# Two of the five column operands of a seven-product feed-forward stage, taken from turned blocks instead of being turned

## The chip, the cores and the metric

The kernel runs on one core of a Trainium2 chip. The metric is the device time of one execution in microseconds (us), the median of several runs. Engines are named as in the profile: PE (matrix products and transposes), DVE (elementwise, two inputs), ACT (elementwise, one input), POOL, and SP, which issues most transfers.

## What is computed

The reference is one layer of a streaming encoder on 1024 tokens of width 1024: a mixer (gated delta rule and a short convolution), then a feed-forward block, then a last norm. The change lies in the feed-forward block:

```
h = rms_norm(x, norm2_w) * (1.0 + scale2) + shift2
x = x + gate2 * ((silu(h @ w_gate) * (h @ w_up)) @ w_down)
```

All values are float32. A product is made of three passes in a 32-bit format that PE takes at one column per step ("fp32r"): each operand is split into a high part (rounded to fp32r) and a low part (the rest), and high by high, high by low and low by high are summed.

## The kernel before

**The stage.** `h @ w_gate` and `h @ w_up` are computed in 11 pairs `p`, each of 256 columns of the two weights. Within a pair the 2 by 2 block product (two halves of the 1024 inputs, two halves of the tokens) is done with seven products instead of eight, in the manner of Strassen and Winograd. The weights give A11, A12, A22 and the sums S1 to S4. The normed tokens, turned so that the inputs lie on partitions, give B11, B21, B22 and T1 to T4:

- T1 = B12 - B11, T2 = B22 - T1, T3 = B22 - B12, and T4 here is B21 - T2.
- The steps of a pair are in the table `STEPS` (line 44): X += A11 B11; Y += A12 B21; X += S2 T2; Z += S1 T1; X += S3 T3; Z += S4 B22; X += A22 T4.
- X, Y and Z are PSUM banks, one each for gate (`q` = 0) and up (`q` = 1). `run(p, s, q_)` (line 1798) issues step `s`: for each `q`, 4 blocks of 128 inputs times three passes, so 12 products of 128x512, or 24 for both `q`. Between the steps the banks are read out: `keep` copies a bank with ACT, `close` adds a bank to a kept copy on DVE, `silu` and `act` finish a block.

**How the B and T operands are made.** After the mixer, tokens lie on partitions in eight tiles `x2n[0..7]`, four for each half of the tokens. `norm_tile` norms a tile. `first_half` and `inner_half` (lines 1567, 1576) turn the first four tiles into B11 and B21: PE turns 128x128 blocks into a PSUM bank (four to a bank), ACT makes the high part, DVE the low part (`tr_split`, line 1543). `sums_x(i)` (line 1557) then makes, still on tokens, the sums of T1, T2, T3 and T4 of tile pair `i`, in place, with four DVE operations of 128x512. In the first pair, p = 0, `t_split(n, banks)` (line 1779) turns one of the operands T2, T1, T3, T4, B22 at a time: 16 transposes into four banks, then 4 ACT and 4 DVE operations. All eleven pairs use these operands.

**What sets the order.** From line 1492 on each engine takes its instructions in the order in which the code is written. Lines 2041 to 2085 are the first pair: PE's transposes stand between its steps, and the first pair's weight sums (`sum_n`), high parts (`cast`) and low parts (`low`; `mat` does both for both `q`) stand among them. High and low parts of weights lie in a ring of buffers (`slot`, line 1768). `W[1].load` (lines 2074, 2075) puts the second pair's weights on SP's queue, into space that the tiles `x2n` held.

Of the kernel before, what the change touches and what calls it, by code (L numbers as in the profile page):

```python
# [17 lines left out]
P = 128  # L18
HEAT = (4, 12, 20)
DMA_T = (1.8, 0.9)  # L20
D = 1024
KB = 8
NT = 8
HT = 512
# [22 lines left out]
A_IX = {n: i for i, n in enumerate(("A11", "A12", "S2", "S1", "S4", "S3", "A22"))}  # L47
# [4 lines left out]
def kernel(  # L52
# [25 lines left out]
    class Ordered:  # L78
# [18 lines left out]
    PE, DVE, ACT, POOL, SP = (Ordered(n, e) for n, e in (  # L97
        ("pe", nc.tensor), ("dve", nc.vector), ("act", nc.scalar), ("pool", nc.gpsimd), ("sp", nc.sync)))
# [7 lines left out]
    def nm(s):  # L106
        n_id[0] += 1
        return f"{s}_{n_id[0]}"
# [11 lines left out]
    class Banks:  # L120
# [68 lines left out]
    def dma(out, in_):  # L189
        SP.dma_start(out=out, in_=in_)  # L190
# [76 lines left out]
    for i, t in enumerate(x0):  # L267
        rs, sq, p0, p1 = norm_rs(t, sp, "n1")
# [274 lines left out]
    b2c = cst.tile([P, KB], F32, name="b2c", tag="b2c")  # L543
    db2 = cst.tile([P, 4], F32, name="db2", tag="db2")
# [921 lines left out]
    gp = x2p = b1p = None  # L1466
# [27 lines left out]
    allb = Banks([5, 6, 7, 3, 4, 0, 1, 2])  # L1494
# [4 lines left out]
    pe = seq  # L1499
# [4 lines left out]
    def bank_tile(b, name):  # L1504
        return psp.tile([P, HT], F32, name=nm(name), tag=f"b{b % 8}")
# [3 lines left out]
    x2n = list(x2)  # L1509
# [45 lines left out]
    tm = {}  # L1555

    def sums_x(i, which=(0, 1)):
        lo, hi = x2n[i], x2n[4 + i]
        if 0 in which:
            tm[i] = raw_t()  # L1560
            DVE.tensor_tensor(lo[:, 0:HT], hi[:, 0:HT], lo[:, 0:HT], ALU.subtract)
            DVE.tensor_tensor(tm[i], hi[:, HT:D], lo[:, 0:HT], ALU.subtract)
        if 1 in which:
            DVE.tensor_tensor(hi[:, 0:HT], hi[:, HT:D], hi[:, 0:HT], ALU.subtract)
            DVE.tensor_tensor(lo[:, HT:D], lo[:, HT:D], tm[i], ALU.subtract)

    def first_half(ks):
        for k in ks:
            H[k][0] = tr_split(lambda: h_slot(k, 0), [x2n[i][:, k * P:(k + 1) * P] for i in range(4)], allb.get("tr"), b2c[:, k:k + 1])

    HN = HT // 2
    tq = {n: hp_.tile([P, 2, 2, HN], F32R, name=n, tag=n) for n in ("q1", "q2", "q3")}

    fq = {}

    def inner_half(a):
# [5 lines left out]
        pa, pb = bank[4 + a], bank[6 + a]  # L1582
        if not fq:
# [68 lines left out]
    w_out_tile(5, 1)  # L1652
    keep_x2(5, (1,))
    inner_half(0)
    inner_half(1)
    early_load(0)
    early_load(1)
    sums_x(0)
# [24 lines left out]
    mp = m_ctx.__enter__()  # L1683
# [91 lines left out]
    B = {"B11": [H[k][0] for k in range(4)], "B21": [H[k][0] for k in range(4, 8)]}  # L1775
# [2 lines left out]

    def t_split(n, banks):
        for k in range(4):  # L1780
            def get():
# [5 lines left out]
            c0 = k * P + (HT if n in ("T4", "B22") else 0)  # L1787
            srcs = [tm[i][:, k * P:(k + 1) * P] if n == "T2" else
                    x2n[i + (4 if n in ("T3", "B22") else 0)][:, c0:c0 + P] for i in range(4)]
            col = {"T2": b2c, "B22": b2c, "T3": db2}.get(n)  # L1790
            off = 0 if n == "T3" else 4
            B[n][k] = tr_split(get, srcs, bank_tile(banks[k], "tr"), None if col is None else col[:, off + k:off + k + 1])
# [53 lines left out]
    def cc(p, n):  # L1846
        if p == 0 and n == "p1":
            c[p][n] = [cst.tile([P, HT], F32, name=nm("cc"), tag="ct"),
                       wst.tile([P, HT], F32, name=nm("cc"), tag="aacc", bufs=1)]
        else:  # L1850
# [190 lines left out]
    dma(x2_scr[7], x2[7])  # L2041
    run(0, 0)
    run(0, 1, (0,))
    W[0].sum_n("S1", (0,))
    W[0].sum_n("S2", (0,))
    keep(0, "p1", "X")
    W[0].cast("S2", 0)
    t_split("T2", (6, 7, 4, 5))
    W[0].low("S2", 0)
    run(0, 1, (1,))  # L2050
    W[0].sum_n("S1", (1,))
    W[0].sum_n("S2", (1,))
    W[0].cast("S2", 1)
    W[0].low("S2", 1)
    t_split("T1", (6, 7, 4, 5))
    close(0, "p1", "Y")
    silu(0, "p1")
    run(0, 2, (0,))
    act(0, "p1")
    dma(am_scr[0, A_IX["A11"]], c[0]["p1"][0])  # L2060
    t_split("T3", (6, 7, 4, 5))
    run(0, 2, (1,))
    W[0].mat("S1")
    t_split("T4", (6, 7, 2, 3))
    W[0].sum_n("S3")
    W[0].sum_n("S4")
    run(0, 3, (0,))
    W[0].mat("S3")
# [7 lines left out]
    keep(0, "u2", "X")  # L2076
    run(0, 3, (1,))
    run(0, 4)
    keep(0, "z5", "Z")
    W[0].mat("S4")  # L2080
    for s in (5, 6):
        if s == 5:
            W[0].mat("A22")
        run(0, s)
        block(0, s)
    for p in range(1, NP):
# [156 lines left out]
    for k, (n, i) in enumerate(slots):  # L2243
        ci, s = seq_d[n]
        ps = prod_d(ci, s, i)
# [80 lines left out]
```

## Time and profile before

| what | value |
|---|---|
| median of 3 runs | 1164.13 us (1163.93 to 1164.54) |
| the profiled execution | 1164.59 us |
| its span | 1162.5 us |
| PE busy in the span | 1152.4 us, 99% |
| DVE / ACT busy | 959.1 us (83%) / 563.1 us (48%) |
| the seven steps of the first pair | from 520.42 to 568.33 us in the span |

How to read it: the span runs from the first to the last instruction that the profile records; the execution's own time is 2.1 us longer. In a timeline, a row is a run of equal instructions: its start, the time from the first one's start to the last one's end, how many (x), and in square brackets the engine's idle time before it with what ended it. "acc" is a PSUM bank of X, Y or Z; "tr" a bank of transposes; "hl" a weight's high and low part; "S" and "R" weight sums and raw weights; "T" and "h" the split T and B operands ("h" also the split T1, which takes such a place); "cc" the kept copies; "raw" in the region of the change holds the T2 sums.

### The profile page before, as it was taken

How to read it: one execution, taken by the hardware profiler on the slowest of the kernel's cores; microseconds unless marked ns; L12 is line 12 of the kernel's file. 1: busy time of each engine (PE TensorE's matmuls, PEld its weight loads, DVE VectorE, ACT ScalarE, POOL GpSimd, SP SyncE). 2: the span in 40 equal slices, each digit the busy share in tenths (PEclk: the TensorE clock that was granted, in tenths of full speed). 3: DMA queues.
4: the chain of work that ended last, by engine and by line, in shares of the span. 5: the costliest groups of instructions: out<-in, count | busy, mean ns of one | idle time of the engine just before them, and what ended most of it. 6: DMA issues, size and time to landing. Idle time of an engine off the chain costs nothing.

```text
span 1162.5 us, 16907 instructions
## 1 busy us (share of the span) xinstructions
PE 1152.4 (99%) x5714; PEld 971.4 (84%) x5714; DVE 959.1 (83%) x1807; ACT 563.1 (48%) x1241; POOL 60.1 (5%) x100
## 2 busy tenths in 40 slices
PE   9999999999999999999999999999999999999997
PEld 7888888888888888888888888888888888888886
DVE  6899889899987898678787778777887797688676
ACT  6779633459634552325434433434434465443344
POOL 1110001002101010100000000000000000000002
PEclk9999999999999999999999999999999999999999
DMA  9823455534225455434264456445654599869403
GB/s 361 324 89 104 147 163 152 182 118 148 96 67 172 155 193 179 173 105 140 81 217 139 160 191 217 168 140 182 235 171 151 176 325 394 319 204 340 145 30 145
DMA packets 127542, 209.18 MB, mean 180 GB/s; under 512 B 20576, under 2 KB 45152, under 8 KB 127456
## 3 DMA queue, kind: packets, MB, share of 16 engines
q1 hardware_dynamic: 122080, 204.90, 51.4%
q10 hardware_dynamic: 5376, 3.21, 0.9%
q8 instruction: 45, 0.74, 0.3%
q14 instruction: 41, 0.34, 0.1%
HBM read 153.01 MB, written 55.05 MB: 179 GB/s over the span
## 4 chain that ended last, share of the span: by engine, by line
PE 93%; DVE 3%; ACT 2%; DMA 1%; issue 1%; SPq 0%; POOL 0%; ACTq 0%; DVEq 0%; POOLq 0%
PE acc L89 34%; PE acc L448 25%; PE dn L89 17%; PE o L448 4%; PE o L89 3%; PE A L448 1%; PE K L448 1%; DVE xo L90 1%; PE ab L448 1%; PE O L448 1%; PE kk L448 1%; DVE T L90 0%; PE qk L448 0%; DVE hl L90 0%; DMA raw<-in_w_ada_dram 0%
## 5 line engine op out<-in xcount | busy, mean ns | idle before, releaser
L448 PE MATMUL acc<-h,u 128*128 128x512 f32 x1200 | 298.6, 398 | 0.0
L448 PEld LDWEIGHTS acc<-h,u 128*128 128x128 f32 x1200 | 219.6, 188 | 42.2 <-issue 0.5
L89 PE MATMUL acc<-h,hl 128*128 128x512 f32 x576 | 135.3, 390 | 0.0
L89 PE MATMUL acc<-T,hl 128*128 128x512 f32 x552 | 131.3, 391 | 0.5 <-ACT cc L90 0.5
L89 PEld LDWEIGHTS acc<-h,hl 128*128 128x128 f32 x576 | 107.4, 188 | 21.8
L89 PEld LDWEIGHTS acc<-T,hl 128*128 128x128 f32 x552 | 102.3, 188 | 21.2 <-ACT cc L90 0.9
L89 PE MATMUL acc<-h,u 128*128 128x512 f32 (+1 forms) x480 | 91.8, 341 | 0.0
L90 DVE TENSOR_TENSOR xo<-xo,dn 128x512 f32<-128x512 f32 x84 | 57.1, 685 | 41.5 <-PE dn L89 34.2
L89 PE MATMUL dn<-h,h 128*128 128x512 f32 x396 | 90.7, 389 | 0.0
L89 PEld LDWEIGHTS acc<-h,u 128*128 128x128 f32 x480 | 78.3, 189 | 11.7
L89 PEld LDWEIGHTS dn<-h,h 128*128 128x128 f32 x396 | 74.4, 188 | 15.4
L448 ACT CAST u<-raw 128x512 fp32r<-128x512 f32 x66 | 40.6, 620 | 63.6 <-PE acc L448 62.3
L90 DVE TENSOR_TENSOR cc<-cc,acc 128x512 f32<-128x512 f32 x66 | 41.5, 647 | 32.1 <-PE acc L89 31.5
L448 DVE TENSOR_TENSOR u<-raw,u 128x512 fp32r<-128x512 f32 x82 | 56.1, 686 | 9.0 <-ACT u L448 8.8
L89 PE MATMUL acc<-T,u 128*128 128x512 f32 x240 | 56.0, 390 | 0.0
L90 ACT CAST hl<-S 128x512 fp32r<-128x512 f32 x44 | 25.3, 622 | 61.3 <-DVE S L90 61.3
L448 DVE SCALAR_TENSOR_TENSOR cv<-pr,cols_a,cv 128x512 f32<-128x512 f32 x72 | 53.4, 748 | 0.9 <-ACT cv L448 0.5
L90 ACT CAST h<-rw 128x512 fp32r<-128x512 f32 x57 | 32.7, 618 | 41.7 <-PE dn L89 34.6
L89 PEld LDWEIGHTS acc<-T,u 128*128 128x128 f32 x240 | 45.1, 188 | 9.3
L90 ACT ACTIVATE cc<-cc 128x512 f32<-128x512 f32 x33 | 20.9, 632 | 64.2 <-DVE cc L90 63.8
L90 ACT CAST u<-R 128x512 fp32r<-128x512 f32 (+1 forms) x60 | 34.1, 584 | 34.3 <-DVE R L90 34.2
L90 DVE TENSOR_TENSOR hl<-S,hl 128x512 fp32r<-128x512 f32 x44 | 28.5, 688 | 26.9 <-ACT hl L90 26.9
(370 smaller groups left out, 2137.8 us busy)
## 6 DMA issues: line engine op xcount, KB each, us to landing
raw<-in_w_in_dram SPq DMA_DIRECT2D x82, 256.0 KB, 3.2
am_scr<-cc SPq DMA_DIRECT2D x77, 256.0 KB, 4.5
raw<-in_w_ada_dram SPq DMA_DIRECT2D x56, 256.0 KB, 3.3
rw<-am_scr SPq DMA_DIRECT2D x55, 256.0 KB, 5.2
rw<-bm_scr SPq DMA_DIRECT2D x53, 256.0 KB, 5.3
bm_scr<-raw SPq DMA_DIRECT2D x51, 256.0 KB, 5.5
R<-in_w_gate_dram SPq DMA_DIRECT2D x22, 512.0 KB, 3.9
R<-in_w_up_dram SPq DMA_DIRECT2D x22, 512.0 KB, 5.3
```

Of the source, the lines that this page charges most:

```text
L89: return call(*a, **k)
L90: ins = call(*a, **k)
L448: ins = call(*a, **k)
```

## The change

T3 and T4 are no longer summed on tokens and turned. They are summed from operands that are turned anyway, since T3 = T2 - B11 and T4 = B21 - T2 hold for turned blocks as well.

- `keep_raw` (new, called in `first_half` and after `inner_half`): ACT copies the eight PSUM banks of the turned B11 and B21, without the shift, to SBUF: B11 by way of `kb` buffers (from which `sums_x` moves it on with another ACT copy), B21 into the right halves of `x2n[0..3]`.
- `sums_x`: two DVE operations of a tile pair instead of four, and that ACT copy.
- `t_split` only turns (T2, T1, B22); its ACT and DVE work is now in `t_turned`, which for T2 also copies the four turned banks to SBUF (into `tm`, the buffers of the T2 sums).
- `t_sums` makes T3 and T4 in SBUF (4 DVE operations each), `t_parts` splits them (4 ACT and 4 DVE operations each, as before, but out of SBUF).
- The first pair's weight sums S1, S2 and S4 are made for gate and up together ahead of the split parts, and the parts are made one `q` at a time with `part`.
- The copies of u2's start (`keep(0, "u2", "X")`) go to a buffer of their own and stand earlier; `act(0, "p1")`, and the store of its result, stand later, behind T4's parts.

```
     def sums_x(i):
         lo, hi = x2n[i], x2n[4 + i]
+        tm[i] = raw_t()
+        DVE.tensor_tensor(lo[:, 0:HT], hi[:, 0:HT], lo[:, 0:HT], ALU.subtract)
+        DVE.tensor_tensor(tm[i], hi[:, HT:D], lo[:, 0:HT], ALU.subtract)
+        ACT.copy(hi[:, 0:HT], b11[i])
+        kept[i] = hi[:, 0:HT]
-            DVE.tensor_tensor(hi[:, 0:HT], hi[:, HT:D], hi[:, 0:HT], ALU.subtract)
-            DVE.tensor_tensor(lo[:, HT:D], lo[:, HT:D], tm[i], ALU.subtract)
+    def keep_raw(ks, banks):
+        for k, ps in zip(ks, banks):
+            if k < 4:
+                b11.append(gp.tile([P, HT], F32, name=f"kb{k}", tag=f"Tt{k}", bufs=1))
+                ACT.copy(b11[k], ps)
+            else:
+                kept[k] = x2n[k - 4][:, HT:D]
+                ACT.copy(kept[k], ps)
...
+        if n == "T2":
+            for k in range(4):
+                ACT.copy(tm[k], t_ps[n, k][0])
+    def t_sums(n):
+        for k in range(4):
+            if n == "T3":
+                DVE.scalar_tensor_tensor(kept[k], tm[k], db2[:, k:k + 1], kept[k], ALU.add, ALU.subtract)
+            else:
+                DVE.tensor_tensor(tm[k], kept[4 + k], tm[k], ALU.subtract)
+    def t_parts(n):
+        for k in range(4):
+            t = B[n][k] = mp.tile([P, 2, HT], F32R, name=nm(n), tag=f"{n}_{k}", bufs=1)
+            split(kept[k] if n == "T3" else tm[k], t[:, 0], t[:, 1], DVE)
+    def part(n, q):
+        W[0].cast(n, q)
+        W[0].low(n, q)
```

The first pair's order is now the following (before: lines 2041 to 2085 above):

```
    run(0, 1, (0,))
    W[0].sum_n("S1")
    W[0].sum_n("S2")
    keep(0, "p1", "X")
    part("S2", 0)
    part("S2", 1)
    t_split("T2", (6, 7, 4, 5))
    t_turned("T2")
    part("S1", 0)
    run(0, 1, (1,))
    t_split("T1", (6, 7, 4, 5))
    part("S1", 1)
    t_turned("T1")
    close(0, "p1", "Y")
    run(0, 2)
    t_sums("T3")
    silu(0, "p1")
    keep(0, "u2", "X")
    W[0].sum_n("S3")
    part("S3", 0)
    t_parts("T3")
    run(0, 3, (0,))
    part("S3", 1)
    t_sums("T4")
    W[0].sum_n("S4")
    t_split("B22", (6, 7, 2, 3))
    part("S4", 0)
    t_turned("B22")
...
    W[1].load(0)
    W[1].load(1)
    run(0, 3, (1,))
    keep(0, "z5", "Z")
    run(0, 4)
    part("S4", 1)
    part("A22", 0)
    t_parts("T4")
    part("A22", 1)
    act(0, "p1")
    dma(am_scr[0, A_IX["A11"]], c[0]["p1"][0])
    for s in (5, 6):
        run(0, s)
        block(0, s)
```

What stands on the engines, at three places. **PE**, in the first pair behind the first four blocks of step 2 (X of gate += S2 T2). Before, 16 transposes follow (the first five are shown; `tr` is a PSUM bank, `x_4` to `x_6` and `h_1_982` are the second half's token tiles):

```order
L89 MATMUL acc_5446<-T_998_5501,hl_5494 128x512 x3
L89 MATMUL acc_5446<-T_1000_5509,hl_5494 128x512 x3
L89 MATMUL acc_5446<-T_1002_5517,hl_5494 128x512 x3
L89 MATMUL acc_5446<-T_1004_5525,hl_5494 128x512 x3
L89 MATMUL tr_5595<-ident,x_4_4587 128x128
L89 MATMUL tr_5595<-ident,x_5_4588 128x128
L89 MATMUL tr_5595<-ident,x_6_4589 128x128
L89 MATMUL tr_5595<-ident,h_1_982_5426 128x128
L89 MATMUL tr_5603<-ident,x_4_4587 128x128
```

And with the change:

```order
L89 MATMUL acc_5454<-T_1002_5530,hl_5504 128x512 x3
L89 MATMUL acc_5454<-T_1003_5533,hl_5504 128x512 x3
L89 MATMUL acc_5454<-T_1004_5536,hl_5504 128x512 x3
L89 MATMUL acc_5454<-T_1005_5539,hl_5504 128x512 x3
L89 MATMUL acc_5455<-T_1002_5530,hl_5507 128x512 x3
L89 MATMUL acc_5455<-T_1003_5533,hl_5507 128x512 x3
L89 MATMUL acc_5455<-T_1004_5536,hl_5507 128x512 x3
L89 MATMUL acc_5455<-T_1005_5539,hl_5507 128x512 x3
L89 MATMUL acc_5647<-h_1_1012_5584,hl_5546 128x512 x3
```

The up half of step 2 follows at once, and step 3 behind it; the same holds where T4 was turned. **DVE**, ahead of the two additions of `close(0, "z5", "X")`, which read the X banks that step 6 goes on to add to. Before:

```order
L90 SCALAR_TENSOR_TENSOR h_1_1043_5730<-tr_5725,b2c,h_1_1043_5730 128x512
L90 TENSOR_TENSOR hl_5785<-R_5441,hl_5785 128x512
L90 TENSOR_TENSOR hl_5788<-R_5442,hl_5788 128x512
L90 TENSOR_TENSOR hl_5791<-R_5441,hl_5791 128x512
L90 TENSOR_TENSOR hl_5794<-R_5442,hl_5794 128x512
L90 TENSOR_TENSOR cc_5782<-cc_5782,acc_5446 128x512
L90 TENSOR_TENSOR cc_5782<-cc_5782,acc_5447 128x512
```

And with the change:

```order
L90 TENSOR_TENSOR hl_5754<-R_5450,hl_5754 128x512
L90 TENSOR_TENSOR hl_5757<-R_5449,hl_5757 128x512
L90 TENSOR_TENSOR T_1039_5760<-raw_5246,T_1039_5760 128x512
L90 TENSOR_TENSOR T_1040_5763<-raw_5314,T_1040_5763 128x512
L90 TENSOR_TENSOR T_1041_5766<-raw_5395,T_1041_5766 128x512
L90 TENSOR_TENSOR T_1042_5769<-raw_5437,T_1042_5769 128x512
L90 TENSOR_TENSOR hl_5772<-R_5450,hl_5772 128x512
L90 TENSOR_TENSOR cc_5500<-cc_5501,cc_5500 128x512
L90 TENSOR_TENSOR cc_5727<-cc_5727,acc_5454 128x512
L90 TENSOR_TENSOR cc_5727<-cc_5727,acc_5455 128x512
```

T4's four low parts and `act(0, "p1")` (`cc_5500`) now stand ahead of the two additions. **ACT**, behind the turning of T2. Before, the next weight part follows T2's four high parts:

```order
L90 ACTIVATE T_998_5501<-tr_5496,b2c 128x512
L90 ACTIVATE T_1000_5509<-tr_5504,b2c 128x512
L90 ACTIVATE T_1002_5517<-tr_5512,b2c 128x512
L90 ACTIVATE T_1004_5525<-tr_5520,b2c 128x512
L90 CAST hl_5543<-S_5488 128x512
```

And with the change:

```order
L90 ACTIVATE T_1002_5530<-tr_5510,b2c 128x512
L90 ACTIVATE T_1003_5533<-tr_5515,b2c 128x512
L90 ACTIVATE T_1004_5536<-tr_5520,b2c 128x512
L90 ACTIVATE T_1005_5539<-tr_5525,b2c 128x512
L90 COPY raw_5246<-tr_5510 128x512
L90 COPY raw_5314<-tr_5515 128x512
L90 COPY raw_5395<-tr_5520 128x512
L90 COPY raw_5437<-tr_5525 128x512
L90 CAST hl_5546<-S_5494 128x512
```

The four copies of T2's banks stand between its high parts and the high part of S1. On SP, the second pair's four weight loads now stand ahead of the store of `act`'s result, no longer behind it, and they wait for DVE's sums of T4 as well as for PE.

More of the change, by code (lines that the diff above doesn't have):

```diff
@@ L1555, with sums_x @@
     tm = {}
-    def sums_x(i, which=(0, 1)):
+    def sums_x(i):
         lo, hi = x2n[i], x2n[4 + i]
[L1559 to L1563, printed above, removed]
-            DVE.tensor_tensor(hi[:, 0:HT], hi[:, HT:D], hi[:, 0:HT], ALU.subtract)
-            DVE.tensor_tensor(lo[:, HT:D], lo[:, HT:D], tm[i], ALU.subtract)
+        tm[i] = raw_t()
[3 more added lines that the diff above has]
+        kept[i] = hi[:, 0:HT]
+    kept, b11 = {}, []
+    def keep_raw(ks, banks):
[6 more added lines that the diff above has]
+                ACT.copy(kept[k], ps)
     def first_half(ks):
+        banks = []
         for k in ks:
-            H[k][0] = tr_split(lambda: h_slot(k, 0), [x2n[i][:, k * P:(k + 1) * P] for i in range(4)], allb.get("tr"), b2c[:, k:k + 1])
+            banks.append(allb.get("tr"))
+            H[k][0] = tr_split(lambda: h_slot(k, 0), [x2n[i][:, k * P:(k + 1) * P] for i in range(4)], banks[-1], b2c[:, k:k + 1])
+        keep_raw(ks, banks)
     HN = HT // 2
@@ L1574 @@
     fq = {}
+    hb = {}
     def inner_half(a):
@@ L1582, in inner_half @@
         pa, pb = bank[4 + a], bank[6 + a]
+        hb.update(bank)
         if not fq:
@@ L1655 @@
     inner_half(1)
+    keep_raw(range(4, 8), [hb[k] for k in range(4, 8)])
     early_load(0)
@@ L1780, in t_split, with get @@
         for k in range(4):
-            def get():
+            def get(k=k):
                 if n == "T1":
@@ L1786, in get, with t_turned @@
                 return mp.tile([P, 2, HT], F32R, name=nm(n), tag=f"{n}_{k}", bufs=1)
-            c0 = k * P + (HT if n in ("T4", "B22") else 0)
+            c0 = k * P + (HT if n == "B22" else 0)
             srcs = [tm[i][:, k * P:(k + 1) * P] if n == "T2" else
[L1789 to L1792, printed above, removed]
+                    x2n[i + (4 if n == "B22" else 0)][:, c0:c0 + P] for i in range(4)]
+            ps = bank_tile(banks[k], "tr")
+            for i, src in enumerate(srcs):
+                pe("pe", PE.transpose(ps[:, i * P:(i + 1) * P], src, ident))
+            t_ps[n, k] = ps, get
+    def t_turned(n):
+        for k in range(4):
+            ps, get = t_ps[n, k]
+            B[n][k] = dst = get()
+            hi, lo = dst[:, 0, :], dst[:, 1, :]
+            if n == "T1":
+                split(ps, hi, lo, DVE)
+            else:
+                col = b2c[:, 4 + k:5 + k]
+                ACT.activation(hi, ps, AF.Identity, bias=col, scale=1.0)
+                DVE.scalar_tensor_tensor(lo, ps, col, hi.bitcast(F32), ALU.add, ALU.subtract)
+        if n == "T2":
+            for k in range(4):
+                ACT.copy(tm[k], t_ps[n, k][0])
+    t_ps = {}
+    def t_sums(n):
+        for k in range(4):
+            if n == "T3":
+                DVE.scalar_tensor_tensor(kept[k], tm[k], db2[:, k:k + 1], kept[k], ALU.add, ALU.subtract)
+            else:
+                DVE.tensor_tensor(tm[k], kept[4 + k], tm[k], ALU.subtract)
+    def t_parts(n):
+        for k in range(4):
+            t = B[n][k] = mp.tile([P, 2, HT], F32R, name=nm(n), tag=f"{n}_{k}", bufs=1)
[3 more added lines that the diff above has]
+        W[0].low(n, q)
     W = {0: Weights(0)}
@@ L1849, in cc @@
                        wst.tile([P, HT], F32, name=nm("cc"), tag="aacc", bufs=1)]
+        elif p == 0 and n == "u2":
+            t = mp.tile([P, 2, HT], F32, name=nm("cc"), tag="L", bufs=1)
+            c[p][n] = [t[:, 0], t[:, 1]]
         else:
@@ L2043 @@
     run(0, 1, (0,))
-    W[0].sum_n("S1", (0,))
-    W[0].sum_n("S2", (0,))
+    W[0].sum_n("S1")
+    W[0].sum_n("S2")
     keep(0, "p1", "X")
-    W[0].cast("S2", 0)
+    part("S2", 0)
+    part("S2", 1)
     t_split("T2", (6, 7, 4, 5))
-    W[0].low("S2", 0)
+    t_turned("T2")
+    part("S1", 0)
     run(0, 1, (1,))
[L2051 to L2054, printed above, removed]
     t_split("T1", (6, 7, 4, 5))
+    part("S1", 1)
+    t_turned("T1")
     close(0, "p1", "Y")
+    run(0, 2)
+    t_sums("T3")
     silu(0, "p1")
[L2058 to L2064, printed above, removed]
-    W[0].sum_n("S3")
+    keep(0, "u2", "X")
+    W[0].sum_n("S3")
+    part("S3", 0)
+    t_parts("T3")
+    run(0, 3, (0,))
+    part("S3", 1)
+    t_sums("T4")
     W[0].sum_n("S4")
-    run(0, 3, (0,))
-    W[0].mat("S3")
     t_split("B22", (6, 7, 2, 3))
+    part("S4", 0)
+    t_turned("B22")
     x2_ctx.__exit__(None, None, None)
@@ L2075 @@
     W[1].load(1)
-    keep(0, "u2", "X")
     run(0, 3, (1,))
+    keep(0, "z5", "Z")
     run(0, 4)
-    keep(0, "z5", "Z")
-    W[0].mat("S4")
+    part("S4", 1)
+    part("A22", 0)
+    t_parts("T4")
+    part("A22", 1)
+    act(0, "p1")
+    dma(am_scr[0, A_IX["A11"]], c[0]["p1"][0])
     for s in (5, 6):
-        if s == 5:
-            W[0].mat("A22")
         run(0, s)
```

## The prediction

> **What bounds the kernel now.** I read the page first, for the engine that bounds and the chain that ended last:
>
> ```profile
> PE 1152.4 (99%) x5714; PEld 971.4 (84%) x5714; DVE 959.1 (83%) x1807; ACT 563.1 (48%) x1241; POOL 60.1 (5%) x100
> ...
> PE 93%; DVE 3%; ACT 2%; DMA 1%; issue 1%; SPq 0%; POOL 0%; ACTq 0%; DVEq 0%; POOLq 0%
> ```
>
> PE has work nearly all the time and holds 93% of the chain. So time taken from PE's queue is time taken from the kernel, as long as PE finds its operands ready. Next, PE's timeline over the first pair:
>
> ```profile
> 528.62 1.91 PE L89 MATMUL tr<-ident,raw 128*128 128x128 f32 x16
> 530.28 2.98 PE L89 MATMUL acc<-h,hl 128*128 128x512 f32 x12
> 533.11 1.91 PE L89 MATMUL tr<-ident,x 128*128 128x128 f32 x16
> 534.77 2.98 PE L89 MATMUL acc<-T,hl 128*128 128x512 f32 x12
> 537.60 0.49 PE L89 MATMUL tr<-ident,x 128*128 128x128 f32 x3
> ...
> 539.35 3.00 PE L89 MATMUL acc<-T,hl 128*128 128x512 f32 x12
> 542.19 1.91 PE L89 MATMUL tr<-ident,x 128*128 128x128 f32 x16
> 543.86 3.02 PE L89 MATMUL acc<-h,hl 128*128 128x512 f32 x12
> ...
> 551.85 5.76 PE L89 MATMUL acc<-T,hl 128*128 128x512 f32 x24 [0.50 <-ACT cc L90]
> 557.45 5.60 PE L89 MATMUL acc<-h,hl 128*128 128x512 f32 x24
> 562.89 5.60 PE L89 MATMUL acc<-T,hl 128*128 128x512 f32 x24
> 568.33 5.60 PE L89 MATMUL acc<-h,hl 128*128 128x512 f32 x24
> ```
>
> The transposes at 528.62 are T2's, at 533.11 T1's, at 537.60 T3's, at 542.19 T4's; steps 4, 5 and 6 start at 551.85, 557.45 and 562.89. PE waits once, 0.50 us, for the copies of u2's start. From start to start, 24 products in a stream take 5.44 us (562.89 to 568.33), so 12 take 2.72. The clock is full in both stretches, so it is no term:
>
> ```profile
> 520.40:535.00 14.60, 14.60 (x82) 12.56 (x81) 11.35 (x17) 4.84 (x9) 0.76 (x2) 1.00 0.45 145
> ...
> 552.00:574.00 22.00, 22.00 (x98) 18.18 (x98) 15.31 (x24) 8.89 (x17) 0.00 (x0) 1.00 0.23 86
> ```
>
> **What the change takes from PE.** T3's turning goes (537.60 to 539.35, 1.75 us) and T4's (542.19 to 543.86, 1.67): 3.42 us. A step that is cut in two by a turning loses a little more: 12 products took 2.83 us (534.77 to 537.60) and 2.84 (539.35 to 542.19) instead of 2.72, so 0.11 each, 0.22. The copy of u2's start moves ahead, which takes away the 0.50 and the slow restart behind it (551.85 to 557.45 is 5.60 instead of 5.44), 0.16, and some 0.15 in front of it. That makes about 4.5 us if PE never waits: steps 2 and 3 start at 534.77 as before; 0.11, then 36 products (8.16), B22's turning (1.66), 12 products (2.83), steps 4 and 5 (10.88) bring step 6 to **558.4** instead of 562.89.
>
> **What it adds elsewhere: DVE is then too late.** The rows that carry this:
>
> ```profile
> 526.57 0.68 DVE L90 TENSOR_TENSOR h<-h 128x512 f32<-128x512 f32 x1
> 527.17 0.69 DVE L90 TENSOR_TENSOR x<-x,raw 128x512 f32<-128x512 f32 x1
> 527.77 0.69 DVE L90 TENSOR_TENSOR S<-R,R 128x512 f32<-128x512 f32 x1
> ...
> 530.46 2.73 DVE L90 SCALAR_TENSOR_TENSOR T<-tr,b2c,T 128x512 fp32r<-128x512 f32 x4 [1.27 <-ACT T L90]
> 533.10 0.68 DVE L90 TENSOR_TENSOR hl<-S,hl 128x512 fp32r<-128x512 f32 x1
> ...
> 536.41 2.48 DVE L90 TENSOR_TENSOR h<-tr,h 128x512 fp32r<-128x512 f32 x4
> ...
> 549.43 1.28 DVE L90 TENSOR_TENSOR hl<-R,hl 128x512 fp32r<-128x512 f32 x2
> ...
> 558.91 1.28 DVE L90 TENSOR_TENSOR cc<-cc,acc 128x512 f32<-128x512 f32 x2
> ```
>
> ```profile
> 529.74 2.42 ACT L90 ACTIVATE T<-tr,b2c 128x512 fp32r<-128x512 f32 x4
> ...
> 542.33 1.15 ACT L90 CAST hl<-S 128x512 fp32r<-128x512 f32 x2
> ...
> 551.20 2.06 ACT L90 COPY cc<-acc 128x512 f32<-128x512 f32 x4
> ```
>
> Slots from start to start: a DVE operation of two tensors 0.60 us ((2.48 - 0.68)/3), one with a column besides 0.66 ((2.73 - 0.74)/3); an ACT high part out of PSUM 0.58, a copy out of PSUM 0.49, a high part out of SBUF 0.53. The operations of T3's sums (two SBUF tensors and a column) have no row here; the nearest are the 0.74 above and, out of SBUF,
>
> ```profile
> L448 DVE SCALAR_TENSOR_TENSOR cv<-pr,cols_a,cv 128x512 f32<-128x512 f32 x72 | 53.4, 748 | 0.9 <-ACT cv L448 0.5
> ```
>
> so 0.66 a slot holds; the bounds are 0.60 and 0.75. T4's sums are plain two-tensor operations: 0.60, at most 0.72 (below).
>
> The chain, on the clock of the trace of before:
> 1. T2 is turned at 528.62 as before. Ahead of it on DVE the last tile's two sums go (526.57 and 527.17), and the sums S1 and S2 take four slots instead of two; S2's second is done at 529.05 and its high part on ACT at about 529.7. So T2's high parts start at **529.7**, where they were (529.74).
> 2. ACT: four high parts (to 532.0), the four new copies (2.0, to 534.0), then S1's high part (0.62). DVE, which until then has only T2's low parts, can take up S1's low part at **534.6**.
> 3. From there DVE has one unbroken queue to `close(0, "z5", "X")`: the low parts of S1 (2) and T1 (4), the two additions of p1, T3's sums (4), S3's (2), S3's low parts (2), T3's low parts (4), T4's sums (4), S4's (2), S4's low parts (2), B22's (4), A22's (2), T4's (4), and `act` (1). That is 31 at 0.60 and 8 at 0.66, 23.9 us. It waits three times for a high part that ACT can only make when the sum is done or B22's parts are through: 0.16 for S3, 0.16 for S4 and 0.56 for S4's second, 0.9 in all.
> 4. The first addition of the close starts at 559.4 and ends at 560.1. Step 6 adds on to the bank that it reads, so PE starts step 6 at **560.1**, not 558.4: a wait of 1.2 to 1.7 us that was not there (before, the close started at 558.91, four us ahead of step 6). Step 5 waits too, some 0.6 us for the copy of Z's start behind B22's high parts on ACT (553.5), but that lies inside the same delay.
>
> Sum: 562.89 - 560.1 = 2.8, less 0.16 for the restart behind a wait: **2.6 us**. Behind the wait in the close stand only the second addition, `act` and pair 1's low parts; DVE is then about one us later than before and PE 2.6 earlier, against six us between A11's first low part at 561.1 and its step at 565.7, so nothing is late there.
>
> **Edits costed at nothing, and their cover.** The eight copies of the first half (ACT has 13.28 us of work in the 36.90 before 520.40) push four early weight loads back: the last copies wait for DVE's last read of these banks, and the loads, issued from 492.78, now leave at about 499.8 to 501.5.
>
> ```profile
> 498.04 0.76 DVE L90 TENSOR_TENSOR qf<-tr,qf 128x256 f32<-128x256 f32 x2
> ```
>
> ```profile
> 492.78 0.39 ACTq L90 DMA_DIRECT2D er<-in_w_gate_dram  x1
> ...
> 514.36 0.62 ACT L90 CAST hl<-er 128x512 fp32r<-128x512 f32 x1 [1.72 <-PE o L89]
> ```
>
> ```profile
> u<-in_w_up_dram ACTq DMA_DIRECT2D x1, 256.0 KB, 4.8
> ```
>
> At 4.8 us to landing they are there at 506.5, and are first read at 514.36: eight us of cover. Pair 1's four loads on SP, issued from 543.91, now wait for T4's sums on DVE (547.0 to 549.4):
>
> ```profile
> 543.91 0.38 SPq L90 DMA_DIRECT2D R<-in_w_gate_dram  x1
> ```
>
> ```profile
> DMA to landing us min/median/max: 3.8/4.8/8.2
> ```
>
> At the longest, 8.2, the last is there at about 558.5, seven us before PE's step on A11. T1's turning at 533.11 waits for the copies of T2's four banks; the first is done at 532.6, the last at 534.1, each before its bank's turn (0.42 apart): 0 to 0.3, which the close's delay swallows.
>
> [...] A transpose in the trace:
>
> ```profile
> L89 PE MATMUL tr<-ident,x x88: 270/273/328, 483.5 to 548.2; 128*128 128x128 f32 x88
> ```
>
> [...]
>
> The low parts out of PSUM (536.41, four in 2.48) and out of SBUF (549.43, two in 1.28) both come every 0.60 us, so taking T3 and T4 from SBUF shortens nothing. [...]
>
> **The rivals.**
> - *PE never waits*: if ACT's copies overlap better and DVE is up to 1.7 us earlier at the close. 4.5 us gained, 1159.6. For it: two slots of DVE work per tile are gone ahead of T2. Against it: step 2 of the chain hangs on ACT, not on those slots.
> - *The queue is somewhat longer*: waits that I set at 0.9 are 2, or ACT starts T2 later, each us lost one for one. A gain of 0.8 to 2.3, so about 1162.5.
> - *The dearer slot* (slower than before): a DVE operation whose operand comes straight from the one before takes 0.72 instead of 0.60:
>
> ```profile
> 507.02 0.68 DVE L90 TENSOR_TENSOR x<-x,x 128x512 f32<-128x512 f32 x1
> 507.74 0.69 DVE L90 TENSOR_TENSOR raw<-x,x 128x512 f32<-128x512 f32 x1
> ```
>
>   Were all 31 so spaced, the close would come 3.7 us later and step 6 at 563.8: 1.1 us slower, 1165.2. It decides from 0.68 a slot on. Against it: in the new order none of the 31 reads what its neighbour just wrote.
> [...]
>
> **The numbers.** The profiled execution took 1164.59 us, 2.1 more than its span and 0.46 more than the median; 2.6 less is 1162.0 for it, and **1161.5** from the median. Chances: the forecast (2.3 to 3.4 us gained) 0.54, PE never waits 0.12, the longer queue 0.25, the dearer slot or any other loss 0.07, the transpose at its duration 0.02. The range leaves out the dearer slot and the 1155.3, and reaches from 1159.8 to 1163.6. A measurement of this kernel can tell about 0.2%, 2.3 us: faster than 1161.8 is likely by 0.62, within by 0.32, slower by 0.06.
>
> **What would show it.** PE: two turnings fewer, step 2 in one piece of 5.5 us from 534.8, no wait of step 4 for a copy, and instead a wait of 1 to 1.7 us at step 6 put down to DVE's cc. DVE: no idle of note from S1's low part to the close, which starts around 559.4. If step 6 doesn't wait, my queue is too long; if PE waits at step 2 or 3, or at pair 1's first steps, my cover was wrong.

## The result, and the profile after

The changed kernel takes 1162.25 us (median of 22 runs, 1160.92 to 1163.58) against 1164.14 (median of 22 runs, 1163.37 to 1165.00): a ratio of 0.9984, 95% interval 0.9978 to 0.9991, so 1.9 us faster, by 1.0 to 2.6. The forecast was 1161.5. The profiled execution of the changed kernel took 1163.06 us, 0.8 over its own median. That will matter below.

The page of the changed kernel: 32 matmuls fewer (5682 instead of 5714), and the chain that ended last holds less PE and more DVE and DMA.

```profile
PE 1149.2 (99%) x5682; PEld 967.1 (83%) x5682; DVE 957.9 (83%) x1807; ACT 571.5 (49%) x1257; POOL 59.5 (5%) x100
...
PE 90%; DVE 4%; ACT 2%; DMA 2%; issue 1%; ACTq 0%; SPq 0%; POOL 0%; DVEq 0%
```

PE's timeline over pair 0 of the changed kernel (start, length, both in us; in brackets the idle time ahead and what ended it). Step 3, from 541.00 to 548.24, with the transposes of B22 inside it, is left out:

```profile
520.21 8.36 PE L89 MATMUL acc<-h,hl 128*128 128x512 f32 x36
528.41 1.91 PE L89 MATMUL tr<-ident,raw 128*128 128x128 f32 x16
530.08 2.98 PE L89 MATMUL acc<-h,hl 128*128 128x512 f32 x12
533.57 2.12 PE L89 MATMUL tr<-ident,x 128*128 128x128 f32 x16 [0.51 <-ACT raw L90]
535.44 5.72 PE L89 MATMUL acc<-T,hl 128*128 128x512 f32 x24
...
548.24 5.60 PE L89 MATMUL acc<-T,hl 128*128 128x512 f32 x24
554.74 5.74 PE L89 MATMUL acc<-h,hl 128*128 128x512 f32 x24 [0.90 <-ACT cc L90]
561.38 5.72 PE L89 MATMUL acc<-T,hl 128*128 128x512 f32 x24 [0.90 <-DVE cc L90]
566.94 5.60 PE L89 MATMUL acc<-h,hl 128*128 128x512 f32 x24
```

T3's and T4's turnings are gone, step 2 runs in one piece, and step 4 (548.24) waits for nothing. In their place PE waits three times: at T1's turning for the copies of T2's banks, at step 5 for the copy of Z's start, at step 6 for DVE's close. DVE in the same execution:

```profile
526.11 0.68 DVE L90 TENSOR_TENSOR S<-R,R 128x512 f32<-128x512 f32 x1
528.17 0.69 DVE L90 TENSOR_TENSOR S<-R,R 128x512 f32<-128x512 f32 x1 [1.38 <-DMA R<-in_w_up_dram]
528.78 1.29 DVE L90 TENSOR_TENSOR S<-S,R 128x512 f32<-128x512 f32 x2
...
535.53 1.29 DVE L90 TENSOR_TENSOR hl<-S,hl 128x512 fp32r<-128x512 f32 x2 [1.45 <-ACT hl L90]
...
556.94 2.49 DVE L90 TENSOR_TENSOR T<-raw,T 128x512 fp32r<-128x512 f32 x4
559.35 0.68 DVE L90 TENSOR_TENSOR hl<-R,hl 128x512 fp32r<-128x512 f32 x1
559.95 0.68 DVE L90 TENSOR_TENSOR cc<-cc,cc 128x512 f32<-128x512 f32 x1
560.55 1.27 DVE L90 TENSOR_TENSOR cc<-cc,acc 128x512 f32<-128x512 f32 x2
```

The new thing is the second row: the second of S1's two sums waits 1.38 us for a weight load. (The first is that of gate, the second that of up; the texts below call them the two halves.) The forecast had not counted on that. ACT passes the delay on: T2's high parts start at 530.62, 10.41 us behind pair 0's first product (forecast 529.7, which is 9.28 behind it), and the copies behind them end too late for T1's turning. Further down, ACT stands 4.3 us at S4's high part, with B22's high parts and the copy of Z's start queued behind it:

```profile
530.62 2.42 ACT L90 ACTIVATE T<-tr,b2c 128x512 fp32r<-128x512 f32 x4
532.91 2.06 ACT L90 COPY raw<-tr 128x512 f32<-128x512 f32 x4
...
551.27 0.62 ACT L90 CAST hl<-R 128x512 fp32r<-128x512 f32 x1 [4.30 <-PE acc L89]
551.80 2.42 ACT L90 ACTIVATE h<-tr,b2c 128x512 fp32r<-128x512 f32 x4
554.09 1.09 ACT L90 COPY cc<-acc 128x512 f32<-128x512 f32 x2
```

This row names PE, but what S4's high part waits for is its sum on DVE. In a second profile of the same kernel the sums of S4 and the same wait read:

```profile
549.41 1.28 DVE L90 TENSOR_TENSOR R<-R,S 128x512 f32<-128x512 f32 x2
...
550.26 0.62 ACT L90 CAST hl<-R 128x512 fp32r<-128x512 f32 x1 [4.30 <-DVE R L90]
```

In both profiles the high part starts 0.16 us after the end of the first of S4's sums (550.42 + 0.69 in the first, 549.41 + 0.69 in the second), and these sums stand behind T4's four sums in DVE's queue.

**One measure for all runs.** The start of pair 0 (the x36 row) lies between 519.37 and 521.27 us in the executions below, whatever the kernel: that is jitter of the work ahead of it. What follows pair 0, the profiled time less the start of pair 1, is 595.9 to 596.4 us in all of them. So I compare the **length of pair 0**, from its first product to the first of pair 1: before, 568.33 - 520.42 = 47.91; changed, 566.94 - 520.21 = 46.73. All starts of steps below are counted from pair 0's first product too. Each ratio comes from all runs of both kernels in its own series, in which the medians before are 1164.14 to 1164.30, so it isn't quite the quotient of two medians of the table; changed_again2 is a single execution.

| kernel | median us | ratio to before (95%) | profiled us | step 5 starts | step 6 starts | length of pair 0 |
|---|---|---|---|---|---|---|
| before | 1164.14 | | 1164.59 | 37.03 | 42.47 | 47.91 |
| changed, first profile | 1162.25 | 0.9984 (0.9978-0.9991) | 1163.06 | 34.53 | 41.17 | 46.73 |
| changed_again | 1162.09 | 0.9981 (0.9972-0.9989) | 1162.03 | 33.26 | 39.90 | 45.46 |
| changed_again2 | | | 1161.14 | 33.38 | 40.02 | 45.55 |
| sums_by_half | 1162.30 | 0.9984 (0.9975-0.9993) | 1162.89 | 34.12 | 40.75 | 46.31 |
| z5_first | 1161.12 | 0.9973 (0.9962-0.9983) | 1162.01 | 32.54 | 39.08 | 44.61 |
| close_first | 1160.80 | 0.9968 (0.9956-0.9981) | 1160.36 | 33.28 | 38.86 | 44.32 |
| low_twice | 1164.29 | 0.9997 (0.9988-1.0006) | 1162.24 | 33.18 | 41.28 | 46.82 |
| loads_late | 1163.55 | 0.9999 (0.9990-1.0007) | 1164.17 | 35.06 | 41.70 | 47.25 |
| t3_only | 1161.26 | 0.9974 (0.9963-0.9985) | 1161.26 | 34.30 | 39.74 | 45.18 |
| t4_only | 1162.28 | 0.9980 (0.9971-0.9989) | 1163.52 | 35.18 | 40.62 | 46.06 |
| sums_alone | 1163.45 | 0.9992 (0.9984-1.0001) | 1163.45 | 36.07 | 41.51 | 46.95 |
| all_but_s1 | 1160.55 | 0.9968 (0.9956-0.9981) | 1161.45 | 32.54 | 38.85 | 44.42 |
| all_moves | 1159.76 | 0.9961 (0.9949-0.9974) | 1159.07 | 32.54 | 38.25 | 43.77 |

### The profile page after: what moved, and what is told of

Its sections match the earlier page's. It is cut to its first block, busy times and chain, and to the rows that moved or that the text cites. A ratio compares the mean times of both kernels' runs of the same rounds, so it can differ in the third digit from the quotient of the medians.

```text
span 1161.1 us, 16878 instructions
## 1 busy us (share of the span) xinstructions
PE 1149.2 (99%) x5682; PEld 967.1 (83%) x5682; DVE 957.9 (83%) x1807; ACT 571.5 (49%) x1257; POOL 59.5 (5%) x100
## 4 chain that ended last, share of the span: by engine, by line
PE 90%; DVE 4%; ACT 2%; DMA 2%; issue 1%; ACTq 0%; SPq 0%; POOL 0%; DVEq 0%
PE acc L89 33%; PE acc L448 25%; PE dn L89 17%; PE o L448 4%; PE o L89 1%; PE A L448 1%; PE K L448 1%; DMA R<-in_w_up_dram 1%; DVE xo L90 1%; PE ab L448 1%; PE O L448 1%; PE kk L448 1%; DVE x L90 1%; DVE h L90 1%; ACT hl L90 0%
```

## The experiments

**Theory.** PE's gain is 4.5 us; what is missing of it is given back because the work now hangs on the order of DVE's and ACT's queues: the close stands at the end of an unbroken DVE queue, the copy of Z's start stands behind a high part that waits for its sum on DVE (the expectation further down says for its slot, which the rows above don't bear out), and the late weight load shifts all of this in the execution that was profiled. **Rivals:** that the load is the whole loss; that there is simply too much work on DVE, in any order; that each turning is worth its PE time whatever DVE does.

### One part undone: the sums of both halves

```
 W[0].sum_n("S1", (0,)); W[0].sum_n("S2", (0,))      # one half ahead of T2
 part("S2", 0)
 t_split("T2", ...); t_turned("T2")
+W[0].sum_n("S1", (1,)); W[0].sum_n("S2", (1,)); part("S2", 1)   # moved to here
 part("S1", 0)
```

> The changed kernel with one part undone: S1 and S2 are summed for the first column half alone ahead of T2, and for the second half behind T2's low parts, as before the change. Counted from pair 0's first product, the changed kernel starts T1's turning at 13.36 us (0.51 of it a wait), step 5 at 34.53 and step 6 at 41.17. My theory (the DVE queue up to the close, and z5's copy on ACT, set the second half of the pair): DVE no longer waits 1.38 for a weight load, T1's turning starts 0.5 to 0.7 earlier, but S1's high part still stands behind T2's copies and now behind S2's second high part, so step 5 starts at 34.1 with a longer wait of 1.4 and step 6 at 40.8: a gain of 0.3 to 0.4 us, about 1161.9. Rival (the late weight load is the whole loss against my forecast): all steps move by 0.9 or more, step 6 at 40.2, about 1161.3.

PE's rows of this kernel for steps 5 and 6 (pair 0 starts at 520.42):

```profile
554.54 5.75 PE L89 MATMUL acc<-h,hl 128*128 128x512 f32 x24 [1.42 <-ACT cc L90]
561.17 5.72 PE L89 MATMUL acc<-T,hl 128*128 128x512 f32 x24 [0.89 <-DVE cc L90]
```

T1's turning no longer waits, and the waits are where the theory put them: 1.42 at step 5, step 6 at 40.75. Pair 0 is 0.42 shorter than in the first profile of the changed kernel. But the median, 1162.30, is no better than the changed kernel's. The edit takes the load's wait away and at the same time puts S1's high part behind S2's second one, so that S1's low parts start 14.9 us behind pair 0's first product, where the next profile has 14.0. So it can't tell what the load alone costs: the rival (the load is the whole loss against the forecast) stays open here. The next two profiles decide it.

### The changed kernel profiled again

> The changed kernel once more, for a second profile. In its first profile (1163.06 us, 0.8 above its median) DVE waited 1.38 for the last weight load of pair 0, which landed 7.7 us after its issue; in the profiles of the z5 and of the close experiment, which are the same up to there, it did not wait. My theory: the landing differs from execution to execution, and the waits follow it. If DVE doesn't wait here: T1's turning starts without a wait, step 5 waits 0.5 to 0.6 instead of 0.90, step 6 starts at 39.7 to 39.9 us from pair 0's first product, as forecast (39.7), pair 1 at 45.2 to 45.4, and this execution is near 1161.5. If it waits by 1.4 again: step 6 at 41.2. Rival: the wait is in every execution of this kernel, and 41.2 comes out again whatever the load does.

> The changed kernel a third time, for one more profile: the same two outcomes as in the second, 39.7 to 39.9 us for step 6 with no wait of DVE for the load, 41.2 with one of 1.4, and in between in proportion.

PE's rows of the second profile, and below them DVE's (the sums of S1, S1's low parts, the close):

```profile
520.47 8.36 PE L89 MATMUL acc<-h,hl 128*128 128x512 f32 x36
...
533.16 1.91 PE L89 MATMUL tr<-ident,x 128*128 128x128 f32 x16
...
553.73 5.74 PE L89 MATMUL acc<-h,hl 128*128 128x512 f32 x24 [0.56 <-ACT cc L90]
560.37 5.72 PE L89 MATMUL acc<-T,hl 128*128 128x512 f32 x24 [0.90 <-DVE cc L90]
565.93 5.60 PE L89 MATMUL acc<-h,hl 128*128 128x512 f32 x24
```

```profile
526.55 1.28 DVE L90 TENSOR_TENSOR S<-R,R 128x512 f32<-128x512 f32 x2
...
534.51 1.29 DVE L90 TENSOR_TENSOR hl<-S,hl 128x512 fp32r<-128x512 f32 x2 [1.45 <-ACT hl L90]
...
559.54 1.28 DVE L90 TENSOR_TENSOR cc<-cc,acc 128x512 f32<-128x512 f32 x2
```

No wait for the load, none at T1's turning, 0.56 at step 5, step 6 at 39.90 (forecast 39.7). The third profile shows the same, step 6 at 40.02. So the length of pair 0 depends on when this load lands, and against the forecast the rival was nearly right: the load makes 1.27 of the 1.49 us by which step 6 was late in the first profile (41.17 - 39.68). Of PE's 4.5 us some 2 are missing without it too (47.91 - 45.46 is 2.45). From issue to landing the slowest of the four weight loads took, in the first profile and in the second:

```profile
DMA to landing us min/median/max: 3.4/4.1/7.6
```

```profile
DMA to landing us min/median/max: 3.8/4.7/6.2
```

The one execution with 7.6 us lost 1.27 us of pair 0 by it (46.73 - 45.46). Even in time the load has next to no cover: in the second profile it is issued at 520.72 and lands 6.2 us later, at 526.9, and DVE reads it at 527.15. How often it comes late, and why, the runs don't show: only profiled executions tell.

### The load made later on purpose

```
-    for half in (0, 1): W[0].load(half)
+    W[0].load(0)
     dma(x2_scr[7], x2[7])
+    W[0].load(1)
```

> The changed kernel with pair 0's last two weight loads issued behind the store of x2's last tile, which waits for DVE till about 521.7 us, so some 2 us later than now. My theory (with the sums of both halves in one go, this landing sets T2's high parts and all behind them): the last load lands at 529.5 or later, T1's turning waits 1.5 to 2.5 instead of 0.51, step 6 starts 1 to 2 us later than in the changed kernel's first profile (41.17), and the time is 1.0 to 2.3 over the changed kernel's median, 1163.3 to 1164.6. Rival (the load's landing is covered and the 1.38 wait was swallowed by the queue behind it): the same time as the changed kernel, within 0.4.

DVE's sums of S1 in this kernel, and below them PE's turning of T1:

```profile
527.80 0.69 DVE L90 TENSOR_TENSOR S<-R,R 128x512 f32<-128x512 f32 x1 [1.20 <-DMA R<-in_w_gate_dram]
529.23 0.69 DVE L90 TENSOR_TENSOR S<-R,R 128x512 f32<-128x512 f32 x1 [0.74 <-DMA R<-in_w_up_dram]
```

```profile
534.64 2.12 PE L89 MATMUL tr<-ident,x 128*128 128x128 f32 x16 [1.03 <-ACT raw L90]
```

Here both sums wait, since `load(1)` brings a part that each of them reads. DVE waits 1.94 in all; pair 0 is 1.79 longer than in the second profile, the median 1.3 to 1.5 over the changed kernel's two. The interval now includes the time before (0.9990 to 1.0007): a load two us later takes most or all of the gain. The load landed at about 529.1 and not at 529.5 or later, my number for T1's turning, 1.5 to 2.5, was too high (1.03), and step 6 came 0.5 later than in the first profile, not 1 to 2; against an execution without a wait, 1.8. The rival (covered) falls.

### The order ahead of the close, both ways

The close moved ahead of two DVE operations (the store of p1's product moves with them):

```
 part("A22", 0); t_parts("T4")
-part("A22", 1); act(0, "p1")
 run(0, 5); block(0, 5)        # the close of z5 is in here
+part("A22", 1); act(0, "p1")
 run(0, 6)
```

> The changed kernel with A22's second part and the product of p1 moved behind the close of z5, so two DVE operations of 0.60 us leave the queue ahead of the close. My theory (step 6 waits for the close because of the order on DVE): the close starts 1.2 earlier, step 6's wait of 0.90 and the slow restart behind it go, step 6 starts at 39.9 to 40.1 instead of 41.17, step 5 keeps its wait: a gain of 1.1, about 1161.2. Rival (step 6 waits for T4's low parts, or for the bank in some other way, and the close only happens to end then): no gain.

PE's rows for steps 5 and 6 of this kernel:

```profile
553.11 5.75 PE L89 MATMUL acc<-h,hl 128*128 128x512 f32 x24 [0.58 <-ACT cc L90]
558.69 5.62 PE L89 MATMUL acc<-T,hl 128*128 128x512 f32 x24
```

And two operations more ahead of it, A22's low part made three times over:

```
 part("A22", 0)
+W[0].low("A22", 0)
+W[0].low("A22", 0)
 t_parts("T4")
```

> The changed kernel with two DVE operations more ahead of the close of z5: the low part of A22's first half is made three times over instead of once, 0.60 us each. My theory (step 6 waits for the close at the end of an unbroken queue): the close and step 6 come 1.2 later, one for one, 1163.4; together with the run in which the close has two operations fewer ahead of it, a slope of one on both sides of the changed kernel. Rival (DVE has slack there): no change.

DVE's low parts of S4 and A22 in this kernel, four in a row:

```profile
553.65 2.75 DVE L90 TENSOR_TENSOR hl<-R,hl 128x512 fp32r<-128x512 f32 x4 [0.47 <-ACT hl L90]
```

and PE's step 6 in the same execution:

```profile
560.76 5.71 PE L89 MATMUL acc<-T,hl 128*128 128x512 f32 x24 [2.36 <-DVE cc L90]
```

With two fewer, step 6's wait is gone and step 5 keeps its own: step 6 comes at 38.86, 1.04 ahead of the second profile's 39.90. With two more the close starts 40.45 us behind pair 0's first product instead of 39.07, and step 6 comes at 41.28 instead of 39.90: both 1.38 later. (The numbers 39.9 to 40.1 of the first text were counted from the profile with the late load.) So the close's place in DVE's queue sets step 6: one for one where it waits, up to the 0.9 and the restart that there was to win. The rivals fall. Open in the second is its median, 1164.29, 0.9 above the theory's 1163.4: four executions, the profiled one among them, took 1162.2 to 1163.0, seven 1163.6 to 1165.4. Six of these seven show a granted clock of 0.997, where all other executions on record show 0.998 or 0.999. I have no profile of one, so what made them longer isn't shown, and the slope rests on the profiles alone.

### Z's copy ahead of the waiting high part

```
 t_split("B22", ...)
-part("S4", 0)
 t_turned("B22")
 ...
 keep(0, "z5", "Z")
+part("S4", 0)
 run(0, 4)
```

> The changed kernel with S4's first part moved behind z5's copies, so that on ACT B22's high parts and z5's copies no longer stand behind a high part that waits for its slot. My theory: the wait of 0.90 us at step 5's start goes (step 5 at 33.4 instead of 34.53), some of it comes back inside step 5 because S4's low part now stands behind B22's on DVE, and DVE loses its two waits of 0.22 and 0.48, so step 6 starts at 40.2 to 40.4 instead of 41.17 and still waits for DVE: a gain of 0.8, about 1161.4. Rival 1 (DVE's work alone sets step 6): gain under 0.3. Rival 2 (z5's copy is a loss of its own): the gain is 0.90 and the restart behind it, 1.1.

PE's rows for step 5 (in two pieces) and step 6:

```profile
553.81 0.61 PE L89 MATMUL acc<-h,hl 128*128 128x512 f32 x2
554.84 5.28 PE L89 MATMUL acc<-h,hl 128*128 128x512 f32 x22 [0.42 <-DVE hl L90]
560.35 5.69 PE L89 MATMUL acc<-T,hl 128*128 128x512 f32 x24 [0.23 <-DVE cc L90]
```

Step 5 starts without a wait, loses 0.42 two products later because S4's low part now comes behind B22's, and step 6 waits 0.23. Pair 0 is 0.85 shorter than in the second profile, the median 1.1 under the changed kernel's. The theory gave 0.8 and the second rival 1.1: pair 0 says the first, the median the second, and the rows, in which 0.42 and 0.23 come back as waits, speak for the theory. Step 6 came at 39.08 and not at 40.2 to 40.4, since those two numbers were counted from a profile with the late load. The first rival (under 0.3) falls.

### Half the change at a time

In one, T4 is turned as before and only T3 is made by columns; in the other the reverse. Each has one turning of 1.67 us and one cut more on PE than the changed kernel, and four sums fewer in DVE's queue up to the close, since they are made ahead of T2 as before. The operand that is turned again also gets its high and low parts right behind its turning, and the copies of B21's or B11's banks, which only its sum by columns needs, fall away.

> Half of the change: T3 is made by columns, T4 by transposes as before the change (right behind step 2, its sums ahead of T2, no copies of the second half's banks). PE has one turning and one cut more than the changed kernel, 1.78 us. My theory (the second turning's gain was given back whole by the DVE queue): without T4's four sums on DVE no step from 3 on waits, pair 1 starts at 46.2 us from pair 0's first product (changed kernel 46.73), about 1161.9, not slower than the changed kernel. Rival (each turning is worth its PE time): 1.8 slower than the changed kernel, about 1164.0.

> The other half: T4 by columns, T3 by transposes inside step 2 as before the change. My theory, as for the other half: no wait from step 3 on, pair 1 starts at 46.1 instead of 46.73, about 1161.9. Rival (each turning is worth its PE time): 1.8 slower than the changed kernel, about 1164.0.

PE of the kernel with T3 alone by columns (T4's turning, then steps 5 and 6):

```profile
539.96 1.91 PE L89 MATMUL tr<-ident,x 128*128 128x128 f32 x16
...
554.37 5.60 PE L89 MATMUL acc<-h,hl 128*128 128x512 f32 x24
559.81 5.60 PE L89 MATMUL acc<-T,hl 128*128 128x512 f32 x24
```

No step waits, and with 16 transposes more its median, 1161.26, is 0.8 to 1.0 under the changed kernel's two; with T4 alone by columns it is 1162.28, the same as theirs, with no wait from step 3 on, and one of 0.45 at T1's turning in its profile. The theory's 1161.9 for both lies between the two. The rival forecast 1164.0 for both and falls. By the profiles, taking away T4's turning as well makes pair 0 0.28 longer (45.18 to 45.46), and taking away T3's as well makes it 0.60 shorter (46.06 to 45.46), where PE saves 1.78 either way. So the second turning that the change removes brings little or nothing in this order: most of PE's 1.78 us come back as waits for DVE and ACT.

### The sums alone, on the kernel before

> The kernel before with one part of the change alone: S1 and S2 of both column halves in one go ahead of T2; all five operands are turned. My theory: DVE waits for the second half's weight load and T2's high parts come 0.9 late, but nothing on PE hangs on that yet; S2's second high part no longer waits for its sum, ACT gets through T1's and T3's parts sooner, and step 4's wait of 0.50 for u2's copies goes: 0.5 to 0.8 faster than before, about 1163.5. Rival (the sums in one go cost what the late load costs): T1's turning waits 0.5 or more, 0.3 to 0.9 slower than before, about 1164.7.

PE's step 4 of this kernel (pair 0 starts at 520.15):

```profile
550.78 5.60 PE L89 MATMUL acc<-T,hl 128*128 128x512 f32 x24
```

Step 4 starts without its wait of 0.50, pair 0 is 0.96 shorter and the median 0.7 to 0.85 lower than before (interval to 1.0001, so just short of certain). The load landed in time here, and DVE did not wait for it as the theory had said. ACT's row for S2's second high part, in the kernel before and in this one:

```profile
535.14 0.62 ACT L90 CAST hl<-S 128x512 fp32r<-128x512 f32 x1 [2.98 <-DVE S L90]
```

```profile
532.23 0.64 ACT L90 CAST hl<-S 128x512 fp32r<-128x512 f32 x1
```

Part of the change's gain is thus none of the turnings': this high part no longer waits for its sum, and u2's copies, which stand where they stood before, end in time. The rival (T1's turning waits) falls.

### All moves together

Besides the three moves above, S4's low part goes ahead of B22's low parts, and S1's first high part ahead of T2's copies on ACT. The second kernel leaves that last move out.

> The changed kernel with all of these moves: sums by half, S4's first part and B22's low parts behind z5's copies with S4's low part first, the close ahead of A22's second part and p1's product, and besides S1's first high part ahead of T2's copies on ACT. My theory: no step of pair 0 waits any more by over 0.2; step 5 starts at 32.7, step 6 at 38.2 and pair 1 at 43.7 instead of 46.73, a gain of 2.8 to 3.0 on the changed kernel, about 1159.4, which is what my forecast gave for a PE that never waits. Rival (DVE has too much work in this stretch in any order): DVE is the bound whatever stands first, waits come back at steps 5 or 6, and the gain is 1.5 at most, about 1160.8.

> The kernel with all moves, less one: S1's first high part stands behind T2's four copies on ACT, as in the changed kernel. My theory (the length of DVE's queue from S1's low part to the close counts one for one): DVE starts on S1 some 2 us later than in the kernel with all moves, of which the second half's sums fill 0.6 to 1.2; step 6 waits 0.6 to 0.8 for the close again, pair 1 starts at 44.3 (all moves: 43.7), about 1160.0. Rival (ACT's order there is covered): as fast as with all moves, within 0.2.

PE's steps 5 and 6 and pair 1's first, in the kernel with all moves:

```profile
551.91 5.60 PE L89 MATMUL acc<-h,hl 128*128 128x512 f32 x24
557.62 5.69 PE L89 MATMUL acc<-T,hl 128*128 128x512 f32 x24
563.14 5.60 PE L89 MATMUL acc<-h,hl 128*128 128x512 f32 x24
```

and step 6 in the one without the last move:

```profile
559.80 5.73 PE L89 MATMUL acc<-T,hl 128*128 128x512 f32 x24 [0.69 <-DVE cc L90]
```

With all moves step 6 is 0.27 late (557.62 - 551.91 - 5.44) and nothing else waits: 1159.76 us, 0.9961 of the time before (0.9949 to 0.9974). Without the last move the wait of 0.69 for the close is back and pair 0 is 0.65 longer, so the rival that ACT's order there is covered falls. The rival (too much work on DVE in any order) falls too: DVE has the same operations in the changed kernel and in this one. The gain on the changed kernel, 2.3 to 2.5 us by the medians, is a little under the theory's 2.8 to 3.0, which was counted from the profile with the late load.

## Why the forecast came out as it did, step by step

- **PE's gain of 4.5 us** was right. The kernel with all moves shows it nearly whole: pair 0 is 4.14 shorter, and 0.27 of the rest is its last wait. One term had the right size and not the right cause: the 0.81 at step 4 (0.50, 0.16 and 0.15) was put down to the earlier place of u2's copies, and it comes without that when the sums alone are moved.
- **Step 2 of the chain** (S1's low part at 534.6 on the clock of before) held in the second profile: 534.51, at a start of pair 0 that is 0.05 later. In the first it was 535.53, at a start 0.21 earlier.
- **The queue**, 23.9 of work and 0.9 of waits, 24.8 to the close: 25.03 (534.51 to 559.54). Step 6 was forecast for 560.1, 39.68 from pair 0's first product, and came at 39.90 and 40.02. Step 5's wait, forecast 0.6, was 0.56 and 0.68; step 6's own, forecast 1.2 to 1.7, was 0.90 and 0.86. The forecast for the profiled execution, 1162.0 us at a start of pair 0 of 520.42, is what the second profile shows: 1162.03 at 520.47.
- **The step that failed** is the first of the chain: "S2's second is done at 529.05". It counted four slots on DVE and not the load that the second of them reads, the sum of S1's second half, which the change moves ahead by some 6.5 us (533.70 before, 527.17 in the forecast's order). The trace of before could have told: its last weight load lands 0.7 us too late for that.

```profile
520.67 0.50 SPq L90 DMA_DIRECT2D R<-in_w_up_dram  x1
```

```profile
DMA to landing us min/median/max: 3.6/4.1/7.2
```

  Issued at 520.67 and landed after 7.2 us, it is there at 527.9. I had quoted landings of up to 8.2 us and weighed them for pair 1's loads, not for these. Where the load lands after 7.6 us instead of 6.0 to 6.2, T2's high parts start some 1.2 us late (10.41 us behind pair 0's first product, against 9.13 and 9.26) and pair 0 takes 1.3 longer. This is shown for one execution and by the kernel with late loads. That it makes the whole difference between the forecast 1161.5 and the medians 1162.25 and 1162.09 is not shown, since the share of such executions isn't known. An estimate from the profiles (pair 0 starts at 520.3 on average, 596.1 us follow it) makes these medians a pair 0 of 45.7 to 45.9 us, between the 45.46 with the load in time and the 46.73 with the late one.
- **T1's turning**, forecast to wait 0 to 0.3: nothing with the load in time, 0.51 with the late one.
- **The covers** that I had written down held. The four early weight loads were issued at 498.6 to 500.2, and pair 1's from 549.36, and PE waited for neither. Between pair 1's first low part and its step I had written six us; my own two numbers, 561.1 and 565.7, give 4.6, and the first profile shows 5.2 (561.75 to 566.94).
- **The rivals.** PE does wait (the first falls). The measured gain, 1.9 us, lies below the forecast's band of 2.3 to 3.4 and in that of the longer queue, 0.8 to 2.3, to which I had given half the chance. A longer delay is what the first profile shows, by a cause that I hadn't named; the second profile shows the forecast's own queue. The dearer slot didn't come: T4's low parts follow each other every 0.60 us ((2.49 - 0.69)/3). A slot of that size shows up in one of the experiments, for another kind of dependence: where an operation overwrites what the one before wrote, in the kernel with A22's low part three times over, four take 2.75; if only the two gaps between those that write the same tile are longer, they are 0.73 rather than 0.60 ((2.75 - 0.69 - 0.60)/2).
- **Transposes, and where the low parts come from.** In a stream a transpose costs PE 0.104 us (16 from 528.62 to 530.28 in the trace of before), not its duration of 273 ns: with 32 fewer and next to no wait left, the kernel with all moves has a pair 0 that is 4.14 us shorter, and not the 8.7 that 32 times 273 ns make. The 1155.3 that the forecast's range leaves out, and the chance of 0.02, take each transpose to cost PE its duration; no run shows that. And low parts out of SBUF are no shorter than out of PSUM: T4's four took 2.49 us from SBUF, and 2.48 from PSUM before the change (at 544.63).
- **PE's time by columns.** "One column per step" is, in the trace of before, 0.44 ns a column: 24 products of 512 columns take 5.44 us from start to start (562.89 to 568.33). Twelve of 256 columns take 1.43 (762.76 to 764.19), 0.47 ns a column.

## What to carry to other kernels

When work is taken from the engine that bounds, write down the next engine's queue in program order up to each wait, and put what releases the first one (here the close) ahead of what is read later: here the same operations in another order took the gain from 1.9 us to 4.4. When an operation is moved ahead, look up when the data that it reads lands, at the longest landing in the trace and not at the median; here the trace of before had one that was too long, 7.2 us against a median of 4.1. And where executions jitter by as much as the effect (here the start of pair 0 by 1.9 us, 519.37 to 521.27), compare one stretch of the trace, from one fixed row to another, in two or three profiles.

## What the runs showed of the hardware that I had not expected

The slowest of pair 0's four weight loads, 512 KB each, took 6.0 to 6.3 us to land in twelve of the fourteen profiles, 7.2 in that of before, where nothing waited for it, and 7.6 in the first of the changed kernel, where it made pair 0 1.3 us longer. What makes it late isn't shown. And in the one kernel that has the case, a DVE operation that overwrites the tile of the one before comes 0.73 us behind it instead of 0.60, by the estimate above from four in 2.75 us.
